# A planner's clock: other prices for the matrix products that set the order of two transformer blocks

## The chip, the cores and the metric

The kernel runs on one core of a Trainium2 chip. The metric is the device time of one execution in microseconds (us); a lower number is better. Engines are named as the profile names them: PE (matrix products; PEld is its weight load), DVE (element-wise work), ACT (activations, scaled copies), POOL (a few small operations) and SP, whose queue issues the loads.

## The reference

The input is 256 tokens of 1024 values in float32. Two blocks follow each other, each of two layers.

```python
def first_block(x, mem, ...):
    h = x
    for l in range(DEPTH):
        h = h + 0.5 * swiglu_ffn(rms_norm(h, ffn1_norm[l]), ffn1_w_in[l], ffn1_w_out[l])
        h = h + hybrid_mixer(rms_norm(h, mix_norm[l]), w_in[l], conv_w[l], ..., w_out[l])
        h = h + memory_cross_attention(rms_norm(h, xattn_norm[l]), rms_norm(mem, mem_norm[l]), ...)
        h = h + 0.5 * swiglu_ffn(rms_norm(h, ffn2_norm[l]), ffn2_w_in[l], ffn2_w_out[l])
    return rms_norm(h, final_norm)

def second_block(x, ...):                      # each layer:
    ...
    merged = g[:, :, 0] * y_moba + g[:, :, 1] * y_nsa + g[:, :, 2] * y_fox
    return x + merged @ w_out
```

The mixer of the first block has eight heads of stick-breaking attention and four heads of a gated delta rule (GDN) in chunks of 64 tokens, whose inputs pass a causal convolution. A layer of the second block has three attention branches: MoBA, NSA and FoX. NSA compresses keys and values: windows of 32 tokens pass a small network, `silu(flat @ w1) @ w2`. FoX needs a running sum of the logarithms of its forget gates.

## The kernel before, in words

All weights come from DRAM in float32 and are split into a high and a low part of the type f32r: ACT copies the high part (`wh<-raw`), DVE subtracts it from the raw value (`wl<-raw,wh`). Activations are split in the same way (for instance `uh`, `ul`). A dense product is three f32r matmuls, high by high, high by low and low by high (`mm3`, lines 603 to 605, and `chunk_T`, 623 to 628). Most have 256 columns (`pq`), those of the second block's inputs up to 512; the ones that the prediction speaks of have 384 (`pp`). Between these dense products stands side work: transposes (`pt`), sums and broadcasts by constant matrices (`rb`, `cum`), the attentions, the GDN chunks and the norms. Most of its matmuls on PE are float32.

The order on every engine is made by one planner when the program is built (class `Plan`, lines 205 to 335). It keeps a clock for each engine (`free`) and the planned time at which each tile is written (`note`, `ready`). The work of PE in order of the layers is a list; `dense` (598) runs one main product and then lets the side work go on. Each piece of side work is a generator that yields operations. An operation of DVE or ACT is emitted once its planned ready time and its engine's planned free time are near enough (`when`, 173; SLACK 0.25, QUEUE 0.6), a product of PE once 0.6 us have passed since its planned ready time (`PE_SLACK`). "Now" is the planned clock of PE. So what a product is priced at decides how many products are placed between a chain's operations. `until` and `wait` let the planned clock run on where the main product itself isn't ready; `hidden` (1710) waits in this way for the compressed windows `fs`.

The prices: a product has `c` of line 417, a transpose 0.11 us (423), DVE and ACT about 0.1 us plus the elements over a rate (`cost`, 246). Every operation goes through `Op.run` (185 to 193), so all rows of the profile carry line 193; after the change it is line 198.

Names in the rows: `fs` are the windows for NSA's compression, made from `kv` by a transpose (`pt`), DVE (`ft`) and ACT and DVE (`fs`); `hp` is their first product. `hss` are sums of squares of heads. `conv`, `cin` and `gz` belong to the first block's mixer. `fz`, `mz` and `nz` are the gated outputs of the three branches, transposed into `uh` and `ul`, from which `pq` of the branches' output products is made. `p` and `pT` are attention weights, `po` products with values. `lf` are FoX's logarithms, `cum` their running sum.

Of the kernel before, what the change touches and what calls it, by code (L numbers as in the profile page):

```python
# [11 lines left out]
F32R = mybir.dt.float32r  # L12
BF = mybir.dt.bfloat16
# [118 lines left out]
class Xt:  # L132


    def __init__(self, plan, hi, lo):
        self.plan, self.hi, self.lo, self.ready = plan, hi, lo, {}
# [23 lines left out]
class Op:  # L160


    def __init__(self, plan, eng, fn, args, kw, cost, late):
        self.plan, self.eng, self.fn, self.args, self.kw, self.cost, self.late = plan, eng, fn, args, kw, cost, late
        aps = [(i == 0 and "out" not in kw, v) for i, v in enumerate(args) if isinstance(v, bass.AP)]
        aps += [(k in ("out", "accum_out"), v) for k, v in kw.items() if isinstance(v, bass.AP)]
        self.outs = [v for o, v in aps if o]
        self.ins = [v for o, v in aps if not o]

    def ready(self):  # L170
# [14 lines left out]
    def run(self):  # L185
        pl = self.plan
        start = max(pl.free[self.eng], self.ready())
        end = start + self.price()
        pl.free[self.eng] = end
        pl.last = end + self.late  # L190
        for v in self.outs:
            pl.note(v, pl.last)
        return self.fn(*self.args, **self.kw)  # L193
# [13 lines left out]
class Plan:  # L207
# [8 lines left out]

    def __init__(self):
        self.free = {"T": 0.0, "V": 0.0, "A": 0.0, "G": 0.0, "D": 0.0}
        self.heap, self.seq, self.last = [], 0, 0.0
        self.writes = {}  # L220

    @property
# [127 lines left out]
def kernel(ctx: ExitStack, tc: tile.TileContext, a, out):  # L350
    nc = tc.nc
    T = nc.tensor
# [61 lines left out]

    def mm(o, lhsT, rhs, start=True, stop=True, skip=False):
        n = rhs.free_size()
        c = max(n, lhsT.free_size()) * (1 if lhsT.dtype in (F32R, BF) else 4) / 2400.0 + 0.002
        return Op(ck, "T", T.matmul, (), dict(out=o, lhsT=lhsT, rhs=rhs, start=start, stop=stop, skip_group_check=skip),
                  c, 0.2)

# [39 lines left out]
    def late_constants():  # L460
        load(cst[:, C_EARLY:], a["cst"][:, C_EARLY:])

        def run():
            yield V.tensor_tensor(fg, gain("final_norm", 0), gain("norm_g_2", 0), op=OP.mult)
            yield V.tensor_scalar(hbg, C(C_BG, 48), 0.5, None, op0=OP.mult)
            yield V.tensor_copy(idb, ident)
            yield A.activation(tri, C(C_LTN, 2 * P).rearrange("p (i n) -> p i n", i=2), AF.Copy)
            yield V.tensor_copy(sbn, C(C_SBN))
            yield V.tensor_copy(can, C(C_CAN))
        ck.spawn(run(), 0)  # L470
# [132 lines left out]
    def mm3(o, xh, xl, wh, wl, first, last):  # L603
        for lhs, rhs, a0, a1 in ((xh, wh, first, False), (xh, wl, False, False), (xl, wh, False, last)):
            dense(mm(o, lhs, rhs, a0, a1))
# [17 lines left out]
    def chunk_T(ps, n, wh, wl, xh, xl, first, last):  # L623
        for j in range(n // P):
            js = slice(j * P, (j + 1) * P)
            o = ps[j // 2][:, j % 2, :]
            for lhs, rhs, a0, a1 in ((wh, xh, first and j % 2 == 0, False), (wh, xl, False, False), (wl, xh, False, last)):
                dense(mm(o, lhs[:, js], rhs, a0, a1, skip=True))
# [58 lines left out]
    def token_sums(accs):  # L687

        n = len(accs)
        ps = yield from take("x", [P, n, 2], "ssq")  # L690
        for i in range(n):
            for t in range(2):
                yield mm(ps[:, i, t:t + 1], accs[i][:, t * P:(t + 1) * P], one1)
        r = [small("rs", (P, 2), 6) for i in range(n)]
        for i in range(n):
            yield V.tensor_scalar(r[i], ps[:, i, :], 1.0 / D, 0.0 if i else EPS, op0=OP.mult, op1=OP.add)
        give("x")
        return r
# [100 lines left out]
    def to_h(scale, nxt, nx=None):  # L799

        def done(n, ps):
            def run():
                if nx is not None:
                    rb = yield from nx.scale_b()
                for i in range(2):
                    b = 2 * n + i
                    hs = hT[:, 2 * b:2 * b + 2, :]
                    if nx is None:
                        yield V.scalar_tensor_tensor(hs, ps[i], scale, hs, op0=OP.mult, op1=OP.add)
                        give("a")  # L810
                    else:
                        d = k2([P, 2, S], "dh")
                        yield V.scalar_tensor_tensor(d, ps[i], scale, wide(rb), op0=OP.mult, op1=OP.mult)
                        give("a")
                        yield V.tensor_tensor(hs, hs, d, op=OP.add)
                    nxt.start(b)
            ck.spawn(run(), PR_H)
        return done


    def ffn(nx, w_in, w_out, nxt, between=None):
        act = Blocks()

        def block(n0, n):
# [3 lines left out]
            def gate(ps):  # L828
                def run():
                    rb = yield from nx.scale_b()  # L830
                    sg = st["sg"] = [k2([P, 2, S], "sg") for i in range(nk // 2)]
                    for i in range(nk // 2):
                        yield V.tensor_tensor(sg[i], ps[i], wide(rb), op=OP.mult)
                        give("a")
                        yield A.activation(sg[i], sg[i], AF.Silu)
                st["gate"] = ck.spawn(run())
# [1339 lines left out]
```

## Time and profile before

| | us |
|---|---|
| runs, median of three | 1848.15 (1847.22 to 1850.67) |
| profiled execution | 1848.62 |
| its span, first to last instruction | 1846.8 |
| PE busy | 1827.1 (99% of the span), 14854 instructions |
| DVE busy | 1256.0 (68%) |
| ACT busy | 988.2 (54%) |
| chain that ended last | PE 96%, DVE 2%, ACT 1%, issue 1% |

PE's busy time counts overlapping matmuls by their modelled ends: one product of 256 columns is shown with 0.28 us, though the next starts 0.12 us later. Times of single instructions on PE are therefore read from the distance of their starts. "x4" in a row of a timeline means four instructions in succession, and the bracket at its end is the idle time of that engine before them, with what released it. A float32 product that isn't a transpose is two instructions in the trace.

### The profile page before, as it was taken

The page shows a single profiled execution, that of the slowest core. Times are in us where ns is not written, and L with a number is a line of the kernel's source. Part 1 is how long each engine was busy: PE and PEld are TensorE (multiplying, and loading weights), DVE is VectorE, ACT ScalarE, POOL GpSimd, SP SyncE. Part 2 cuts the span into 40 slices and gives each one's busy share as a digit, 9 for nine tenths or more (in the row PEclk, how much of TensorE's full clock was granted, in tenths as well). Part 3 has the DMA queues.
Part 4 walks back from the last instruction along what each step waited for, and adds up shares of the span by engine and source line. Part 5 has one row for each costly group of instructions (what it writes and reads, how often), then busy time and mean ns, then how long its engine had stood idle before and what let it go on. Part 6 is the DMA issues. An engine that isn't in the chain of part 4 may idle for free.

```text
span 1846.8 us, 35541 instructions
## 1 busy us (share of the span) xinstructions
PE 1827.1 (99%) x14854; PEld 1768.2 (96%) x14854; DVE 1256.0 (68%) x2083; ACT 988.2 (54%) x1648; POOL 70.6 (4%) x72
## 2 busy tenths in 40 slices
PE   8999999999999999999999999999999999999999
PEld 8999999899999999999998899999989999999998
DVE  6557687675655565576866666556777868787686
ACT  5446375454544444464654545444576654666553
POOL 0000001000000000000010000000110000101000
PEclk9999999999999999999999999999999999999999
DMA  7546463244554555464632445546535625545533
GB/s 256 183 147 236 144 206 115 92 144 130 183 183 160 188 190 184 146 236 150 203 123 92 137 138 172 184 155 199 168 113 164 234 87 182 166 122 173 198 108 127
DMA packets 169581, 300.90 MB, mean 163 GB/s; under 512 B 7884, under 2 KB 51020, under 8 KB 169292
## 3 DMA queue, kind: packets, MB, share of 16 engines
q1 hardware_dynamic: 169420, 298.63, 50.3%
q8 instruction: 116, 1.90, 0.4%
q14 instruction: 45, 0.37, 0.1%
HBM read 297.56 MB, written 1.05 MB: 162 GB/s over the span
## 4 chain that ended last, share of the span: by engine, by line
PE 96%; DVE 2%; ACT 1%; issue 1%; DMA 0%; POOL 0%; SPq 0%; ACTq 0%; POOLq 0%
PE pq L193 69%; PE pp L193 14%; PE pt L193 2%; PE s L193 1%; PE z L193 1%; PE po L193 1%; PE xs L193 1%; PE xo L193 1%; PE hp L193 1%; DVE wl L193 1%; PE mp L193 1%; PE ep L193 1%; PE sbo L193 1%; ACT wh L193 0%; DMA raw<-in_ffn_w_in_dram 0%
## 5 line engine op out<-in xcount | busy, mean ns | idle before, releaser
L193 DVE TENSOR_TENSOR wl<-raw,wh 128x1024 fp32r<-128x1024 f32 (+3 forms) x628 | 689.3, 1103 | 383.9 <-ACT wh L193 380.9
L193 ACT ACTIVATE wh<-raw 128x1024 fp32r<-128x1024 f32 (+3 forms) x628 | 598.6, 962 | 512.8 <-PE pq L193 384.8
L193 PE MATMUL pq<-ffn_normh,wh 128*128 128x256 f32 x1408 | 399.7, 284 | 0.1
L193 PE MATMUL pq<-ffn_norml,wh 128*128 128x256 f32 x1408 | 399.5, 284 | 0.0
L193 PE MATMUL pq<-ffn_normh,wl 128*128 128x256 f32 x1408 | 399.5, 284 | 0.0
L193 PEld LDWEIGHTS pq<-ffn_normh,wh 128*128 128x128 f32 x1408 | 271.2, 193 | 0.5 <-ACT ffn_normh L193 0.5
L193 PEld LDWEIGHTS pq<-ffn_norml,wh 128*128 128x128 f32 x1408 | 271.2, 193 | 0.0
L193 PEld LDWEIGHTS pq<-ffn_normh,wl 128*128 128x128 f32 x1408 | 271.1, 193 | 0.0
L193 PE MATMUL pq<-ah,wh 128*128 128x256 f32 x704 | 199.5, 283 | 0.0
L193 PE MATMUL pq<-al,wh 128*128 128x256 f32 x704 | 199.5, 283 | 0.0
L193 PE MATMUL pq<-ah,wl 128*128 128x256 f32 x704 | 199.3, 283 | 0.0
L193 PEld LDWEIGHTS pq<-ah,wl 128*128 128x128 f32 x704 | 135.1, 192 | 0.2 <-DVE wl L193 0.2
L193 PEld LDWEIGHTS pq<-al,wh 128*128 128x128 f32 x704 | 135.1, 192 | 0.0
L193 PEld LDWEIGHTS pq<-ah,wh 128*128 128x128 f32 x704 | 135.1, 192 | 0.0
L193 PE MATMUL pp<-wh,norm_g_2l 128*128 128x384 f32 (+3 forms) x352 | 118.9, 338 | 0.0
L193 PE MATMUL pp<-wl,norm_g_2h 128*128 128x384 f32 (+3 forms) x352 | 118.4, 336 | 0.3 <-DVE wl L193 0.3
L193 PE MATMUL pp<-wh,norm_g_2h 128*128 128x384 f32 (+3 forms) x352 | 118.0, 335 | 0.0
L193 PE MATMUL pq<-norm_g_2h,wl 128*128 128x256 f32 x384 | 110.7, 288 | 0.4 <-DVE wl L193 0.4
L193 PE MATMUL pq<-norm_g_2h,wh 128*128 128x256 f32 x384 | 110.5, 288 | 0.0
L193 PE MATMUL pq<-norm_g_2l,wh 128*128 128x256 f32 x384 | 109.7, 286 | 0.0
L193 PE MATMUL pq<-mix_normh,wl 128*128 128x256 f32 x320 | 91.4, 286 | 0.5 <-DVE wl L193 0.5
L193 PE MATMUL pq<-mix_normh,wh 128*128 128x256 f32 x320 | 91.7, 286 | 0.0
(428 smaller groups left out, 3776.5 us busy)
## 6 DMA issues: line engine op xcount, KB each, us to landing
raw<-in_ffn_w_in_dram SPq DMA_DIRECT2D x79, 1024.0 KB, 5.2
raw<-in_w_in_dram SPq DMA_DIRECT2D x48, 1024.0 KB, 5.1
raw<-in_ffn_w_out_dram SPq DMA_DIRECT2D x40, 1024.0 KB, 5.2
raw<-in_w_in_dram SPq DMA_DIRECT2D x28, 768.0 KB, 4.4
raw<-in_xattn_w_kv_dram SPq DMA_DIRECT2D x16, 1024.0 KB, 5.1
raw<-in_w_out_dram SPq DMA_DIRECT2D x16, 1024.0 KB, 5.1
raw<-in_ffn_w_in_dram SPq DMA_DIRECT2D x18, 512.0 KB, 3.7
raw<-in_xattn_w_q_dram SPq DMA_DIRECT2D x8, 1024.0 KB, 5.1
```

Of the source, the lines that this page charges most:

```text
L193: return self.fn(*self.args, **self.kw)
```

## The change

Two prices of PE are altered; nothing that is computed is.

A product's price was the larger of its columns and its weights' columns, over 2400 per us, plus 0.002, with a factor of 4 for float32. Now it is its columns alone, with the same factor, plus 0.014, and at least 0.112. That makes 0.121 from 0.109 for f32r of 256 columns, 0.174 from 0.162 for 384, 0.227 from 0.215 for 512 and for float32 of 128, 0.112 from 0.055 for f32r of 64 to 128 columns with as many weights, and for float32 with 64 columns and 128 of weights 0.121 from 0.215. Besides, each product of PE whose last operand is of another kind (f32r or bfloat16 on the one side, the rest on the other) than that of the product before it is priced 0.06 higher.

```diff
@@ Op.__init__
         self.outs = [v for o, v in aps if o]
+        self.kind = aps[-1][1].dtype
         self.ins = [v for o, v in aps if not o]
@@ Op.run
         end = start + self.price()
+        if self.eng == "T":
+            small = self.kind not in (F32R, BF)
+            end += 0.06 * (small != pl.small)
+            pl.small = small
         pl.free[self.eng] = end
@@ Plan.__init__
-        self.heap, self.seq, self.last = [], 0, 0.0
+        self.heap, self.seq, self.last, self.small = [], 0, 0.0, False
@@ mm
-        c = max(n, lhsT.free_size()) * (1 if lhsT.dtype in (F32R, BF) else 4) / 2400.0 + 0.002
+        c = max(n * (1 if lhsT.dtype in (F32R, BF) else 4) / 2400.0 + 0.014, 0.112)
```

The instructions are the same in number and kind; 631 of the program's products are now priced with the added 0.06. Their order moves throughout. Three places follow.

The first is the first layer of the second block, where the windows of NSA are made. On PE, before:

```order
L193 MATMUL po<-fv,pT 128x128
L193 MATMUL pt<-cst,kv 128x128 x2
L193 MATMUL po<-fv,pT 128x64
L193 MATMUL po<-fv,pT 128x128
L193 MATMUL po<-fv,pT 128x64
L193 MATMUL po<-fv,pT 128x128
L193 MATMUL po<-fv,pT 128x64
L193 MATMUL po<-fv,pT 128x128
L193 MATMUL po<-fv,pT 128x64
L193 MATMUL pt<-cst,kv 128x128 x2
L193 MATMUL hp<-wh,fs 30x256
```

And the same place of PE now, with the dense products `pp` of 384 columns between:

```order
L198 MATMUL pt<-cst,kv 128x128 x2
L198 MATMUL pp<-wh,norm_g_2h 128x384
L198 MATMUL pp<-wl,norm_g_2h 128x384
L198 MATMUL pp<-wh,norm_g_2l 128x384
...
L198 MATMUL pt<-cst,kv 128x128 x2
L198 MATMUL pp<-wh,norm_g_2l 128x384
...
L198 MATMUL hp<-wh,fs 30x256
```

Eight `pp` now stand between the two pairs of `kv` and thirteen between the second and `hp`; the seven `po` stand elsewhere. In the second layer it is eight and seven. On DVE the same place read, before:

```order
L193 TENSOR_TENSOR wl<-raw,wh 128x2x384
L193 TENSOR_TENSOR ft<-pt,cst 64x240 x2
L193 RECIPROCAL sums<-sums 128x2
L193 TENSOR_REDUCE hss<-hsq 128x6
L193 TENSOR_TENSOR fz<-fz,sums 128x128
L193 TENSOR_REDUCE ut<-po 128x128
L193 TENSOR_REDUCE hss<-hsq 128x6
L193 TENSOR_TENSOR fs<-ft,fs 128x16x15
```

And now:

```order
L198 TENSOR_TENSOR wl<-raw,wh 128x2x256
L198 RECIPROCAL sums<-sums 128x2
L198 TENSOR_TENSOR fz<-fz,sums 128x128
L198 TENSOR_REDUCE ut<-po 128x128
L198 TENSOR_SCALAR ngt<-ngt 128x24
L198 TENSOR_TENSOR ft<-pt,cst 64x240 x2
L198 TENSOR_TENSOR fz<-ut,fz 128x128
L198 TENSOR_TENSOR wl<-raw,wh 128x2x256
L198 TENSOR_TENSOR fs<-ft,fs 128x16x15
```

The two `hss` no longer stand between `ft` and `fs`; one `fz` and one `wl` do.

The second place is the first block's mixer, on DVE, from the third weight split of 2x264 on. Before:

```order
L193 TENSOR_TENSOR wl<-raw,wh 128x2x264
L193 SCALAR_TENSOR_TENSOR conv<-cin,cst,conv 128x253
L193 SCALAR_TENSOR_TENSOR conv<-cin,cst,conv 128x254
L193 SCALAR_TENSOR_TENSOR conv<-cin,cst,conv 128x255
L193 TENSOR_SCALAR conv<-cin,cst 128x256
L193 TENSOR_TENSOR wl<-raw,wh 128x2x264
L193 SCALAR_TENSOR_TENSOR conv<-cin,cst,conv 128x253
L193 SCALAR_TENSOR_TENSOR conv<-cin,cst,conv 128x254
L193 TENSOR_TENSOR wl<-raw,wh 128x1024
```

And now:

```order
L198 TENSOR_TENSOR wl<-raw,wh 128x2x264
L198 TENSOR_SCALAR conv<-cin,cst 128x256
L198 SCALAR_TENSOR_TENSOR conv<-cin,cst,conv 128x253
L198 SCALAR_TENSOR_TENSOR conv<-cin,cst,conv 128x254
L198 SCALAR_TENSOR_TENSOR conv<-cin,cst,conv 128x255
L198 TENSOR_SCALAR conv<-cin,cst 128x256
L198 SCALAR_TENSOR_TENSOR conv<-cin,cst,conv 128x253
L198 TENSOR_TENSOR wl<-raw,wh 128x2x264
L198 SCALAR_TENSOR_TENSOR conv<-cin,cst,conv 128x254
L198 TENSOR_TENSOR wl<-raw,wh 128x1024
```

One `conv` stands between the last 2x264 split and that of 1024 where two stood; more of them stand ahead of it. On ACT one `cin` more stands ahead of the high part of that last 2x264 split than before.

The third place is the end of a second-block layer on PE, where the gated outputs are transposed for the branches' output products. Before:

```order
L193 MATMUL pt<-cst,fz 128x128 x3
L193 MATMUL pt<-cst,p 128x128 x4
L193 MATMUL po<-vcat,pT 128x64
...
L193 MATMUL po<-vcat,pT 128x64
L193 MATMUL pq<-uh,wh 128x256
L193 MATMUL pt<-cst,mz 128x128 x3
L193 MATMUL pq<-ul,wh 128x256
```

And now:

```order
L198 MATMUL pq<-norm_g_2h,wh 128x256
L198 MATMUL pq<-norm_g_2l,wh 128x256
L198 MATMUL pq<-norm_g_2h,wl 128x256
L198 MATMUL pt<-cst,fz 128x128 x6
L198 MATMUL pq<-uh,wh 128x256
L198 MATMUL pt<-cst,mz 128x128 x3
L198 MATMUL pq<-ul,wh 128x256
```

The four `p` and the seven `po` (five of them are left out above) no longer stand between the transposes of `fz` and the first `pq` of `uh`.

## Rows read from the trace of the kernel before

**Rows 1.** The page, part 1: busy time, share of the span, instructions.
```profile
PE 1827.1 (99%) x14854; PEld 1768.2 (96%) x14854; DVE 1256.0 (68%) x2083; ACT 988.2 (54%) x1648; POOL 70.6 (4%) x72
```
**Rows 2.** PE's waits by releaser: us in total, times, longest.
```profile
PE pt L193 <- DMA h<-in_x_dram: 7.1, 3, 4.3
PE hp L193 <- DVE fs L193: 2.6, 2, 1.6
PE sp L193 <- DVE vn L193: 1.4, 2, 0.7
PE pt L193 <- DVE ft L193: 0.9, 2, 0.6
PE pq L193 <- DVE wl L193: 0.9, 4, 0.2
PE cum L193 <- DVE lf L193: 0.8, 1, 0.8
PE pt L193 <- DVE pT L193: 0.5, 1, 0.5
PE po L193 <- DVE ut L193: 0.4, 2, 0.2
```
**Rows 3.** Windows: us, busy PE, PEld, DVE, ACT, POOL, PEclk, DMA share, GB/s.
```profile
660.00:720.00 60.00, 60.00 (x503) 60.00 (x502) 39.26 (x47) 28.81 (x35) 0.69 (x1) 1.00 0.57 184
1380.80:1384.20 3.40, 3.40 (x14) 3.37 (x12) 3.33 (x11) 1.83 (x3) 2.84 (x1) 0.51 0.30 54
1418.00:1441.00 23.00, 22.81 (x184) 21.73 (x183) 19.28 (x43) 17.50 (x41) 1.64 (x1) 1.00 0.56 179
```
**Rows 4.** Timeline of PE, first layer of block two: start, us, form, idle before.
```profile
1376.37 0.44 PE L193 MATMUL pt<-cst,kv 128*128 128x128 f32 x2 [0.45 <-DVE pT L193]
...
1378.06 0.41 PE L193 MATMUL pt<-cst,kv 128*128 128x128 f32 x2 [0.55 <-DVE ft L193]
1380.04 0.30 PE L193 MATMUL hp<-wh,fs 128*30 128x256 f32 x1 [1.57 <-DVE fs L193]
```
**Rows 5.** Timeline of DVE at the same place.
```profile
1379.13 0.54 DVE L193 TENSOR_REDUCE hss<-hsq 128x6 f32<-128x384 f32 x1
1379.59 0.40 DVE L193 TENSOR_TENSOR fs<-ft,fs 128x240 fp32r<-128x240 f32 x1
```
**Rows 6.** Timeline of PE, second layer of block two.
```profile
1644.27 0.41 PE L193 MATMUL pt<-cst,kv 128*128 128x128 f32 x2 [0.39 <-DVE ft L193]
1645.73 0.30 PE L193 MATMUL hp<-wh,fs 128*30 128x256 f32 x1 [1.05 <-DVE fs L193]
```
**Rows 7.** Timeline of PE, first norm: the broadcast rb between dense products.
```profile
30.11 0.60 PE L193 MATMUL rb<-cst,rs 128*128 128x128 f32 x4
...
30.67 0.28 PE L193 MATMUL pq<-ffn_normh,wh 128*128 128x256 f32 x1
```
**Rows 8.** Timeline of PE behind the first hp: products of 384 columns.
```profile
1381.12 0.53 PE L193 MATMUL pp<-wh,norm_g_2h 128*128 128x384 f32 x1
...
1384.00 0.46 PE L193 MATMUL pp<-wh,norm_g_2h 128*128 128x384 f32 x1
```
**Rows 9.** Timelines of DVE and ACT in the first mixer.
```profile
239.18 0.71 DVE L193 TENSOR_TENSOR wl<-raw,wh 128x528 fp32r<-128x528 f32 x1 [1.11 <-ACT wh L193]
239.81 0.99 DVE L193 SCALAR_TENSOR_TENSOR conv<-cin,cst,conv 128x253 f32<-128x253 f32 x2
240.75 1.23 DVE L193 TENSOR_TENSOR wl<-raw,wh 128x1024 fp32r<-128x1024 f32 x1
...
239.05 0.71 ACT L193 ACTIVATE cin<-conv 128x256 f32<-128x256 f32 x2
```
**Rows 10.** Timelines of PE and ACT before the first uh of block two.
```profile
1513.28 0.52 PE L193 MATMUL pt<-cst,fz 128*128 128x128 f32 x3
...
1514.77 0.36 PE L193 MATMUL pq<-uh,wh 128*128 128x256 f32 x1
...
1513.84 0.49 ACT L193 ACTIVATE uh<-pt 128x384 fp32r<-128x384 f32 x1 [0.55 <-PE pt L193]
```

## The prediction

> **What bounds the kernel now.** I read the page's busy times first: PE is busy for 1827.1 of the span's 1846.8 us [rows 1]. So the only time to be had is where PE stands, runs at the lower clock, or does other work. The second view was the list of PE's waits by releaser [rows 2]. 7.1 us are the load of x at the start, which the change doesn't touch. Behind it the waits are short and nearly all on DVE: 2.6 us for fs, 1.4 for vn, 0.9 for ft, 0.9 for wl, 0.8 for lf, 0.5 for pT, 0.4 for ut. Third came the table of windows: a stretch of plain dense products runs 503 of them in 60 us at granted clock 1.00, and one stretch of 3.4 us stands at 0.51, half speed [rows 3]. Last I read the timelines at the two longest waits.
>
> Both are at one place, the compressed keys of NSA in the two layers of the second block. In the first layer PE transposes a first pair of kv after a wait of 0.45 us, a second pair after 0.55, and stands 1.57 for fs [rows 4]. Ahead of fs on DVE stand two reductions of hss, the second from 1379.13 [rows 5]. In the second layer the waits are 0.39 and 1.05 [rows 6]. A wait is counted from the modelled end of the matmul before it, which is later than the next could have started: the pair at 1378.06 is two products at a pitch of about 0.11, so hp could have started at 1378.28 and came at 1380.04, 1.76 later instead of the 1.57 shown. The same correction, about 0.17, belongs to each of the five.
>
> **What the change does to the clock.** It computes nothing anew. It alters what the planner believes PE's products to last, and by that the order. Measured pitches are the yardstick.
>
> Products of 256 columns: 60 us over 503 is 0.119 [rows 3]. The old price is 256/2400 + 0.002 = 0.109, the new one 0.121. The old clock ran 9% slow in a plain stretch, so a chain of side work that it gave 2.5 us of products really got 2.76; now it gets 2.49. The first effect, then, is that every hop of a chain has about 0.27 us less cover.
>
> The Trainium skill has a rule on this, "TensorE: Matmul & The Clock Gate", section "Back-to-back issue gap": an isolated product at full clock takes N/2.4 + 2.5 ns. An estimate from it is 109 ns at 256 columns, the old price; by it the old clock was right and the new one runs 10% fast. The trace disagrees, with 0.119 measured, so I give this no chance of its own; it would only make the thinner cover below larger.
>
> Changes of kind: rb, four small f32 products between dense f32r ones, starts at 30.11, one dense product follows it, and the next starts at 30.67 [rows 7]. Four at 0.11 and one at 0.12 make 0.56, all of the distance. The trace has nothing for the 0.06 that the change books at each of two transitions. The order has 631 such changes, so the plan books 38 us that PE doesn't spend, all of it where side work is dense. Those hops lose cover beyond the 0.27.
>
> **The sum, against the profiled execution's 1848.6 us** (the median of the runs is 1848.15, 0.5 lower).
>
> First, kv and hp. The rows of the order show that in the first layer the second pair of kv now stands 13 products of 384 columns ahead of hp, where it stood directly before it, and the first pair 21 ahead. At 0.12 x 384/256 = 0.18 each (an estimate from the 0.119), 21 are 3.7 us of cover beside the transposes. What fs needs from the first pair was 3.5 us before (1376.37 to 1379.9) with two hss of 0.5 ahead of it; the order has taken them away from there, which leaves 2.5. So that wait goes. In the second layer only 15 products stand between the first pair and hp, 2.7 us against the same 2.5: nearly all of it goes. The products that came between, po, run elsewhere at the same cost. Gain: 0.45 + 0.55 + 1.57 + 0.39 + 1.05 = 4.0, with five corrections of 0.17 4.85; I take 0.3 off for the second layer's narrow cover: **-4.55**. Bounds: 0, if DVE's wl ahead of fs comes late each time, to -4.85.
>
> Second, the clock. In the stretch behind the stall the granted clock is 0.51, the lower level of 1.2 GHz [rows 3]. PE had been standing for most of two microseconds. Products of 384 columns are 0.32 apart there, nine of them from 1381.12 to 1384.00 [rows 8], against 0.18: 9 x 0.14 = 1.3. Without the stall it goes: **-1.3** (0 to -1.3; the second layer has the stall and no fall).
>
> Third, the mixers. Before, DVE idles 1.11 at 239.18 for ACT's wh, splits wl of 528, does two conv, and only then the wl of 1024 columns at 240.75 [rows 9] that PE waits for. The order now puts only one conv, 0.40, between the two, and one more cin, 0.33, ahead of that wh on ACT. The wl comes 0.1 to 0.2 earlier, in two mixers: **-0.3**. The bounds are -0.5, two of the 0.2 waits for wl [rows 2], and +0.7, two cin with nothing hidden. The conv moved forward fall into that idle time; without it they cost 0.4 each.
>
> Fourth, lf. PE waits 0.8 for it in one layer [rows 2]. Between that layer's rb and cum the order leaves 27 products of 384 columns instead of 29, so the wait grows by 2 x 0.18: **+0.35** (0, if the chain starts earlier with its rb, to 0.7).
>
> Fifth, uh. Before, three transposes of fz at 1513.28 are followed by four of p and seven po; pq starts at 1514.77, and ACT's uh runs from 1513.84 for 0.49 [rows 10]. Now all six transposes of fz stand directly ahead of pq. These are 0.66 us, and uh needs 0.56 + 0.49 from the first of them: a new wait of 0.4 in each layer. Before, the distance from pq to pq around the transposes behind it already held some of that, so I take half: **+0.45** for both layers (0 to 0.9).
>
> Sixth, thinner cover everywhere else. Nothing in the trace prices it directly. Nine waits of the list [rows 2] (wl, ft, pT, ut) lie between 0.1 and 0.6 and make 2.7 us. If places lie as densely just on the other side, four more turn into waits per 0.27, each by half of it: 0.6. With a little for the 0.06 I take **+0.8**. Bounds: 0, to 0.6 plus all nine growing by 0.27, 3.0.
>
> The two waits for vn stay: the order has the chain of GDN in the same hops. POOL, SP and the loads keep their sequence, and the weight streams are 0.57 busy on DMA in a plain stretch [rows 3]. The number of products of each kind is unchanged.
>
> Sum: -4.55 - 1.3 - 0.3 + 0.35 + 0.45 + 0.8 = -4.55, so 1844.1 in a profile and **1843.5 us** as a median.
>
> **Rivals.**
> A, the gain is handed back: fs comes early, but the thinner cover costs its upper bound, 3.0 instead of 0.8, and uh and lf theirs, 0.9 and 0.7. For it: hops with transposes lose both 0.27 and the unpaid 0.06, and [rows 2] shows how many places lie just late. Against it: no hop lies wholly in islands. Net -4.55 - 1.3 - 0.3 + 0.7 + 0.9 + 3.0 = -1.55, a median of 1846.5.
> B, slower: side work that the fast clock emits earlier lands on DVE ahead of weight splits. The place is the attention of the second block, 1418 to 1441 and its twin in the other layer, where DVE is busy 19.28 of 23 us [rows 3]. Ten per cent of that, 1.9 us, moves ahead of a wl. It decides where the moved work exceeds the idle time directly ahead of that wl: 3.7 us stand in the whole stretch, but spread over several gaps. Then PE waits 1.9 twice, with a half-clock stretch of 1.3 behind each, 6.4, and the mixers' 0.7 + 0.3 come on top: 1843.5 + 7.4 = 1851. For it: PE waits for wl at four places already [rows 2]. Against: DVE's own prices are not altered.
> C, the nearer clock also frees the short waits for wl, ut, pT and ft elsewhere: 0.9 + 0.4 and the 0.8 of lf, with 0.17 on each of seven, and the thinner cover costs nothing: -4.55 - 1.3 - 2.1 - 1.2 = -9.2, 1839.
> D, the change does nothing, because order alone moves and PE's sum is the same: 1848. For it: PE is 99% busy. Against: the waits of fs stand in the trace and the order moves just them.
>
> **How the numbers follow.** Forecast 0.50, A 0.20, B 0.14, C 0.11, D 0.05. A measurement of this kernel tells about 0.2% from no change, 3.7 us. The forecast's own range is 1841.5 to 1845.5, a fifth of it above 1844.45, so faster is 0.40 + 0.11 + 0.02 of A = 0.53; the same is 0.10 + 0.18 + 0.05 = 0.33; slower is 0.14. The range that leaves a tenth on each side reaches from C's 1839, a little below for its unpaid places, to near B: 1838 to 1850.
>
> **What would show it.** In the changed kernel's list of PE's waits hp<-fs should be below 0.5 and the kv transposes gone; there should be no stretch of clock 0.5 behind the first. cum should wait about 1.2, and pq of uh appear with some 0.4. The wait for wl at the mixers should not grow. Wrong would be the sum if PE's waits on wl together exceed 3 us (B), if waits under 0.3 us multiply (A), or if hp still waits over 1 us.

## The result: slower by 1%, and the profile after

The changed kernel takes 1867.9 us in the median of four runs (1866.2 to 1870.6) beside 1848.6 for the one before: a ratio of 1.0104, with an interval of 1.0093 to 1.0116. Forecast were 1843.5 and a range of 1838 to 1850. The prediction was wrong in direction.

The page after, part 1, answers to [rows 1]:

```profile
PE 1836.0 (98%) x14854; PEld 1770.9 (95%) x14854; DVE 1261.4 (68%) x2083; ACT 988.6 (53%) x1648; POOL 70.3 (4%) x72
```

The instructions are as many as before, and the span grew from 1846.8 to 1864.4, so the 17.6 us more are PE standing and PE at the lower clock. The waits of PE answer to [rows 2]; of those up to 0.5 us only the one of cum is shown (us in total, times, longest):

```profile
PE pt L198 <- DMA h<-in_x_dram: 6.9, 3, 4.0
PE qs L198 <- DVE csq L198: 2.7, 2, 1.4
PE pt L198 <- DVE Sn L198: 2.2, 2, 1.1
PE pt L198 <- DVE ul L198: 2.1, 2, 1.0
PE pp L198 <- DVE wl L198: 2.1, 5, 0.8
PE sp L198 <- DVE vn L198: 1.4, 2, 0.7
PE pq L198 <- DVE wl L198: 1.3, 2, 0.6
PE pq L198 <- ACT uh L198: 1.3, 2, 0.6
PE pp L198 <- ACT wh L198: 0.9, 2, 0.4
PE pt L198 <- DVE qh L198: 0.7, 3, 0.2
...
PE cum L198 <- DVE lf L198: 0.3, 1, 0.3
```

The waits of hp for fs and of pt for ft are gone from the list, 3.5 us, and new ones stand in their place. All waits listed make 23.8 us in 36 places, before 15.1 in 19: 8.7 more, and 2.9 more for the 17 additional places at 0.17 each, the correction that the prediction worked out.

The rest is the clock. These windows of the changed kernel (columns as in [rows 3]) stand behind the waits for csq and for ul:

```profile
255.30:258.00 2.70, 2.70 (x13) 2.70 (x14) 1.23 (x1) 0.98 (x2) 0.00 (x0) 0.50 0.00 0
1531.00:1534.00 3.00, 3.00 (x16) 3.00 (x16) 1.62 (x3) 1.01 (x2) 0.00 (x0) 0.52 0.00 0
1800.00:1803.00 3.00, 3.00 (x16) 3.00 (x16) 1.62 (x3) 1.37 (x3) 0.00 (x0) 0.52 0.00 0
1376.00:1384.00 8.00, 8.00 (x59) 7.58 (x57) 7.06 (x20) 5.65 (x17) 0.63 (x1) 1.00 0.33 98
```

Three stretches run at the lower level of 1.2 GHz (0.50 and 0.52); the one that the kernel before had behind hp is gone (last row). The clock doesn't fall in every run of one kernel, so runs are compared below in two parts as well: span times granted clock, an estimate of the time that the span would take at full clock, and the rest. The clock is listed to three places, so a single run's part is good to 0.9 us, a mean of several to less. Before (84 runs, taken beside the experiments): 1843.3 + 3.6. After (4 runs): 1857.1 + 9.3. So about 13.7 us are waits and 5.7 the clock.

Where they arise follows from the starts of the same dense product in both traces, each less the pitches of all products ahead of it. A pitch is the usual distance of two starts where PE neither stands nor runs at the lower clock; the rows are good to some 0.3.

| stretch | us gained (-) or lost |
|---|---|
| up to the first mixer | +0.3 |
| first mixer, projections | +5.5 |
| rest of that layer | +0.6 |
| FFNs between, with the memory's transposes | +0.2 |
| second mixer, projections | +2.4 |
| rest of that layer | +0.6 |
| second block, layer 1, up to the last product ahead of hp | +1.4 |
| from there to hp | -3.0 |
| the clock behind hp | -1.6 |
| from there to the first product of uh | +3.7 |
| the first products of uh | +3.1 |
| layer 2, up to the last product ahead of hp | -0.3 |
| from there to hp | -1.8 |
| from there to the first product of uh | +3.7 |
| the first products of uh | +3.0 |
| the end | -0.2 |

The place that was forecast to gain did so: in layer 1, 4.52 us lay between the starts of the last product ahead of hp and of hp before, and 0.17 lie there now.

```profile
1375.52 0.34 PE L193 MATMUL pp<-wh,norm_g_2l 128*128 128x384 f32 x1
1387.89 0.34 PE L198 MATMUL pp<-wh,norm_g_2l 128*128 128x384 f32 x1
```

### The profile page after: what moved, and what is told of

Read it like the earlier page. It is cut to its first block, busy times and chain, and to the rows that moved or that the text cites. A ratio compares the mean times of both kernels' runs of the same rounds, so it can differ in the third digit from the quotient of the medians.

```text
span 1864.4 us, 35555 instructions
## 1 busy us (share of the span) xinstructions
PE 1836.0 (98%) x14854; PEld 1770.9 (95%) x14854; DVE 1261.4 (68%) x2083; ACT 988.6 (53%) x1648; POOL 70.3 (4%) x72
## 4 chain that ended last, share of the span: by engine, by line
PE 88%; DVE 7%; ACT 2%; issue 1%; POOL 1%; DMA 0%; SPq 0%; POOLq 0%; ACTq 0%
PE pq L198 65%; PE pp L198 11%; PE pt L198 2%; DVE wl L198 2%; PE z L198 1%; PE s L198 1%; DVE conv L198 1%; ACT wh L198 1%; PE po L198 1%; PE xs L198 1%; PE xo L198 1%; PE mp L198 1%; PE ep L198 1%; POOL hss L198 1%; PE sbo L198 1%
```

## The experiments

Where an edit starts from "before" or "after", that is the kernel before or the changed one. F32r products of 256 columns and more are called dense. Ratios are to the kernel before, on the same chip, with 95% intervals.

**Price or fee?** Four kernels. The first two take the change apart.

```diff
# e1_price, from after
-            end += 0.06 * (small != pl.small)
+            end += 0.0 * (small != pl.small)
# e2_fee, from after
-            end += 0.06 * (small != pl.small)
+            end += 0.05 * (small != pl.small)
-        c = max(n * (1 if lhsT.dtype in (F32R, BF) else 4) / 2400.0 + 0.014, 0.112)
+        c = max(n, lhsT.free_size()) * (1 if lhsT.dtype in (F32R, BF) else 4) / 2400.0 + 0.002
# e3_cover, from after
-    PE_SLACK = -0.6
+    PE_SLACK = -0.9
# e5_traced, from e1_price
+        if lhsT.dtype not in (F32R, BF):
+            c = 2 * max(0.11, n / 1200.0)
+            if lhsT.shape[0] <= 64 or lhsT.free_size() <= 64:
+                c = 0.06 if n <= 64 else 0.112
```

> The changed kernel with the new price of products and without the 0.06 for a change of kind. Theory P (the price does the harm: before, products priced 9% too low gave every chain about that much real cover, which made up for what the plan leaves out on ACT and DVE): the waits of the mixers and of uh are all here, the time is 1860 to 1868. Rival F (the fee does the harm: the trace shows no such cost, so the plan's clock runs 38 us ahead where side work is dense): most of the loss is gone, 1846 to 1852. Rival R (any other order costs about this much, since the order before was picked among many): somewhere between 1853 and 1866, with waits at other places than in the changed kernel.

Measured: 1869.3 us, ratio 1.0101 (1.0074 to 1.0128), as slow as the changed kernel, 1 above theory P's range and outside those of F and R.

> The kernel before with its old price of products and a fee for a change of kind, 0.05 instead of 0.06. Theory P: mixers and uh as before, PE waits for kv and hp moved, 1844 to 1851. Rival F: 1858 to 1867, thinner cover wherever side work is dense. Rival R: 1853 to 1866.

Measured: 1847.4, ratio 0.9991 (0.9982 to 1.0001). By itself the fee costs nothing, though by the trace it is false. Theory F falls: without the new prices of products there is no harm. Rival R's range is missed here as well, so not every other order costs that much.

> The changed kernel with PE_SLACK at -0.9 instead of -0.6: side products stand 0.3 us of planned time later on PE. Theory P: this gives back what the nearer price took from hops of 2.5 to 3 us; uh, qs and the short waits of side products go, while the mixers' wait of dense products for wl (an order of ACT and DVE, which PE_SLACK doesn't touch) stays: 1847 to 1853. Rival F: part of it, 1853 to 1860. Rival R: 1853 to 1866 with waits at new places.

Measured: 1861.4, ratio 1.0060 (1.0043 to 1.0077), 1852.1 at full clock and 7.0 for the clock. The cover of side products gave back 5 of the 13.7 us of waits and 2 of the clock. Theory P's number is missed, F's by 1, and R's is met; pp still waits 1.8 for wl, as it said, but so does qs for csq, 2.2, and ul grew to 3.4.

> Prices as the trace has them: f32r as in the changed kernel, float32 of 128 columns 0.22, of 64 rows or columns 0.06 to 0.112, and no fee. Theory P: the mixers' waits (qs for csq, pp for wl and wh) are as in the changed kernel, 8 us; with uh as before, since the order has the seven po between there again: 1855 to 1863. Rival F: the truest clock gives the best order, 1842 to 1848. Rival R: 1853 to 1866, elsewhere.

Measured: 1860.0, ratio 1.0058 (1.0043 to 1.0073). The prices nearest to the trace, without a fee, are slower than the false ones before. Theory P's range holds, and R's with it.

**The mixer's cin.** The trace after shows on ACT what holds up the first mixer:

```profile
234.69 0.65 ACT L198 ACTIVATE wh<-raw 128x528 fp32r<-128x528 f32 x1 [0.73 <-PE pp L198]
236.55 0.42 ACT L198 ACTIVATE cin<-conv 128x256 f32<-128x256 f32 x1 [1.21 <-DVE conv L198]
236.87 2.98 ACT L198 ACTIVATE gz<-pp,rs 64x128 f32<-64x128 f32 x8
239.86 0.42 ACT L198 ACTIVATE cin<-conv 128x256 f32<-128x256 f32 x1
240.19 2.52 ACT L198 ACTIVATE wh<-raw 128x528 fp32r<-128x528 f32 x3
```

and on PE what follows from it:

```profile
240.87 0.39 PE L198 MATMUL pp<-wh,mix_normh 128*128 128x264 f32 x1 [0.45 <-ACT wh L198]
241.61 0.39 PE L198 MATMUL pp<-wl,mix_normh 128*128 128x264 f32 x1 [0.35 <-DVE wl L198]
...
251.53 0.38 PE L198 MATMUL qs<-one,csq 128*128 128x1 f32 x2 [1.36 <-DVE csq L198]
```

One cin has come ahead of the eight gz. It waits 1.21 us for DVE's conv, and gz, wh and wl wait behind it. Before, ACT read here:

```profile
234.35 0.65 ACT L193 ACTIVATE wh<-raw 128x528 fp32r<-128x528 f32 x1 [0.62 <-PE pp L193]
235.49 2.98 ACT L193 ACTIVATE gz<-pp,rs 64x128 f32<-64x128 f32 x8 [0.49 <-PE pp L193]
238.50 0.65 ACT L193 ACTIVATE wh<-raw 128x528 fp32r<-128x528 f32 x1
```

gz itself waited 0.49 for PE there, so not all of the 1.21 is new. Counted from the wh ahead, gz now starts 1.04 later (2.18 for 1.14), and the wh of the last split of 2x264, with a second cin ahead of it, 1.35 later (5.50 for 4.15). wl follows, then DVE's csq, and with the clock behind it the mixer loses 5.5 us. The next kernels add a planner's wait for both halves of conv:

```diff
# x1_cin from after, y4_d012_cin from x2_dense, y3_d006_cin from x5_d006: in conv_done
                         if j % 2:
+                            yield Wait(ck.ready(co[:, j - 1:j + 1, :]) - ck.SLACK)
# x2_dense, from before (x5_d003 and x5_d006: 0.003 and 0.006)
+        if lhsT.dtype == F32R and n >= 256:
+            c += 0.012
```

In three pairs of kernels with the same prices (after and x1_cin, x2_dense and y4_d012_cin, and further below w2_after_oldf32 and w1_x1_oldf32) the edit moves in each of the two mixers two instructions of ACT, so that one cin stands behind gz and another behind a weight split, and five products of PE, among them the first qs; the order of DVE is the same.

> The changed kernel with one more planner's wait in the mixer: the first silu that writes cin is emitted only when both halves of conv are planned ready, so that on ACT it stands behind the eight gz instead of ahead of them. Theory H (in the mixers the harm is one ACT instruction that stands ahead of gz, waits 1.2 us on DVE's conv and holds back gz, wh, wl and csq): the waits of pp for wh and wl and most of qs for csq go, the lower clock behind them too; 1868 falls by 5 to 9, to 1859 to 1863. Rival W (the mixers lose since every weight split has less cover): the waits stay or move, 1866 or more.

Measured: 1862.6, ratio 1.0074 (1.0059 to 1.0089), 5.3 less than the change, in theory H's range; W falls. At full clock 1854.3, 2.7 less; the clock's part is 6.0, 3.3 less. On ACT cin now stands behind gz, which starts without that wait:

```profile
235.16 3.00 ACT L198 ACTIVATE gz<-pp,rs 64x128 f32<-64x128 f32 x8 [0.49 <-PE pp L198]
238.17 0.72 ACT L198 ACTIVATE cin<-conv 128x256 f32<-128x256 f32 x2
```

The waits of pp for ACT's wh are gone, those of qs for csq fell from 2.7 to 1.8 only, and in the run whose trace this is the clock falls in the second mixer instead of the first:

```profile
240.00:300.00 60.00, 59.05 (x578) 55.15 (x579) 50.66 (x89) 31.47 (x60) 6.56 (x6) 1.00 0.50 160
904.00:908.00 4.00, 4.00 (x21) 4.00 (x20) 1.69 (x2) 2.10 (x4) 0.00 (x0) 0.50 0.15 20
```

> The kernel before with 0.012 more on f32r products of 256 columns and more, and nothing else. Theory P (the price of dense products alone sets it): cin stands ahead of gz in the order again and the mixers lose their 7 to 10 us; kv and hp wait less; the end of a layer has po beside uh and loses little: 1855 to 1862. Rival S (the prices of small products matter as much): 1847 to 1852.

Measured: 1853.6, ratio 1.0028 (1.0017 to 1.0039), between the ranges of P and S: 1846.5 and 5.3. The true price of dense products alone brings about a quarter of the loss.

> The kernel before with 0.012 more on dense products, as in x2_dense, and the planner's wait that puts cin behind gz. Theory H: the mixers' waits of pp for wh and wl go; qs may still wait 1 us for csq in each mixer, and where it does the lower clock may follow. 1846 to 1851, from 1853.6. Rival W: no better than x2_dense, 1852 to 1855.

Measured: 1847.9, ratio 0.9996 (0.9987 to 1.0005). In theory H's range; W falls. With the cin back the dense price costs nothing net. It isn't harmless elsewhere: by the reckoning of the table this kernel gains 3.0 and 1.8 at the two hp, as the changed one does, and 0.7 behind the first, and loses most of it again in other places.

**How much, and which small products.** The dense price by half and by a quarter, and the new price for one kind of small products at a time, on the kernel before, on y4_d012_cin and on x5_d006:

```diff
# x3_f32 from before, z3_y4_f32 from y4_d012_cin, y1_d006_f32 from x5_d006
+        if lhsT.dtype not in (F32R, BF):
+            c = max(n * 4 / 2400.0 + 0.014, 0.112)
# x3_r from before, z2_y4_r from y4_d012_cin
+        if lhsT.dtype in (F32R, BF) and n < 256:
+            c = max(n / 2400.0 + 0.014, 0.112)
# y2_after_d006, from after
+        if lhsT.dtype == F32R and n >= 256:
+            c -= 0.006
```

> The same with half of it, 0.006. In the order cin stands behind gz here. Theory H with thresholds (single instructions that change places do the harm): the mixers lose nothing against before, kv and hp wait less, 1845 to 1850. Rival L (thinner cover costs in proportion to the price): about half of x2_dense's loss, 1851 to 1856.

Measured: 1842.7, ratio 0.9968 (0.9955 to 0.9981): faster than both kernels and below the ranges of H and L, 1839.9 at full clock and 0.7 for the clock. Its list of PE's waits:

```profile
PE pt L193 <- DMA h<-in_x_dram: 6.6, 3, 3.8
PE hp L193 <- DVE fs L193: 2.1, 2, 1.1
PE pq L193 <- DVE wl L193: 0.8, 2, 0.4
PE pt L193 <- ACT cin L193: 0.6, 2, 0.3
PE pp L193 <- DVE wl L193: 0.5, 2, 0.3
PE kS L193 <- DVE Sn L193: 0.4, 2, 0.2
PE cum L193 <- DVE lf L193: 0.4, 1, 0.4
```

Besides the load of x these are eleven waits instead of sixteen. hp still waits for fs, yet those of the kv transposes and the lower clock behind hp are gone: by the reckoning of the table 2.0 us of the 5.9 that this trace is shorter lie at the two hp and 1.6 in the clock behind the first. Some 0.7 in each of four other places, the GDN and the uh of both layers, make most of the rest.

> The kernel before with 0.003 more on dense products. Theory H: no harmful place flips in the order (cin behind gz; three fz and then pq of uh, with p and mz behind); kv and hp wait less: 1843 to 1849. Rival L: midway between 1848.4 and the 1842.7 of 0.006, or, if the time is as good as random in the price, outside 1843 to 1849.

Measured: 1849.9, ratio 1.0006 (0.9997 to 1.0016). With 1848.4, 1849.9, 1842.7 and 1853.6 at 0, 0.003, 0.006 and 0.012 the time doesn't follow the price in either direction. So rival L falls in its first form, and theory H's range is missed by 1; what L named last, a time as good as random in the price, is met.

> The kernel before with the new price for float32 products alone (0.012 more for 128 columns, about half for 64 columns with 128 of weights). Theory P: no dense price is altered, the mixers' first place is as before, 1845 to 1852. Rival S: 1854 to 1862.

Measured: 1845.2, ratio 0.9983 (0.9974 to 0.9993), in theory P's range; S falls.

> The kernel before with the new price of small f32r products alone. Theory Q: 1853 to 1860, with waits in the attentions of both blocks. Rival A: 1845 to 1851.

Measured: 1852.6, ratio 1.0026 (1.0015 to 1.0037): between the two, on Q's side.

> y4_d012_cin (dense products 0.012 dearer, cin behind gz; 1847.9) with the new price of f32r products under 256 columns as well. Theory Q (the small f32r price, which holds for the products of the attentions, takes filler away from the tails of the chains): 1855 to 1862. Rival A (only all three prices together make the order with six fz ahead of pq of uh, which isn't in this order): 1846 to 1851.

Measured: 1849.2, ratio 1.0006 (0.9996 to 1.0015), in rival A's range: theory Q falls. The price that cost 4 us on the kernel before costs 1 here.

> y4_d012_cin with the new price of float32 products instead. Theory Q: little changes, 1846 to 1851. Rival A: the same, 1846 to 1851. Rival G (the float32 price, too low by half for products of 64 columns with 128 of weights, makes the loss once the dense price is true): 1854 to 1862.

Measured: 1856.8, ratio 1.0046 (1.0031 to 1.0061). The price that gained 3 us on the kernel before loses 9 here, as rival G said, with the clock's part unchanged (1.9 in both). Part of it is in the GDN, where y4_d012_cin has no such rows:

```profile
PE kS L193 <- DVE Sn L193: 1.8, 2, 0.9
...
PE vp L193 <- DVE X L193: 1.5, 2, 0.7
```

> Two settings that were each faster than before, together: dense products 0.006 dearer and float32 products at the new price. Theory H: the places add up only where they differ; both gain at kv and hp, so 1839 to 1843. Rival (any gain is an accident of one order): 1844 to 1850.

Measured: 1848.8, ratio 0.9997 (0.9987 to 1.0006): two settings that each gained make none together. The rival holds.

> The changed kernel, fee and all, with 0.006 taken off the price of f32r products of 256 columns and more. In the order cin stands behind gz, but the six fz stand directly ahead of pq of uh. Theory H (two places do most of the harm, each by the order of a few instructions): the mixers lose at most 2 us against before; the end of each layer of the second block still loses about 4, with the lower clock behind it; kv and hp gain 2 to 4: 1849 to 1855. Rival L (cover in proportion to the price): half the loss at both places, and the end of a layer not more than 2 each: 1856 to 1860.

Measured: 1857.4, ratio 1.0044 (1.0029 to 1.0059): 1853.7 and 1.9. Most of the clock's part is gone, a quarter of the waits. Theory H's range is missed, and rival L's is met: here taking off half of the dense price takes off about half of the loss. The waits that stay are many and short, though cin stands behind gz.

> x5_d006 (1842.7) with the planner's wait for cin, whose first place differs little in the order. Theory H: within 2 us of x5_d006, 1841 to 1845. Rival (each change of order is as good as random): 1845 to 1852.

Measured: 1845.3, ratio 0.9980 (0.9971 to 0.9989), just outside theory H's range and in the rival's. The edit costs 2.6 where cin stands well already, but it isn't the same small move: here some 45 instructions of DVE change places in the mixers, where none did in the three pairs.

**Do the places add up?** The end of a layer of the second block looks like this after. On PE:

```profile
1526.81 0.82 PE L198 MATMUL pt<-cst,fz 128*128 128x128 f32 x6
1528.26 0.38 PE L198 MATMUL pq<-uh,wh 128*128 128x256 f32 x1 [0.63 <-ACT uh L198]
1529.69 0.55 PE L198 MATMUL pt<-cst,mz 128*128 128x128 f32 x3 [1.04 <-DVE ul L198]
```

and on DVE, where two gt stand ahead of ul:

```profile
1527.48 0.68 DVE L198 TENSOR_TENSOR gt<-pq,rsb 128x512 f32<-128x512 f32 x1
...
1528.28 0.68 DVE L198 TENSOR_TENSOR gt<-pq,rsb 128x512 f32<-128x512 f32 x1
...
1529.08 1.02 DVE L198 TENSOR_TENSOR ul<-pt,uh 128x384 fp32r<-128x384 f32 x2
```

The last two kernels take the old float32 price:

```diff
# w1_x1_oldf32 from x1_cin, w2_after_oldf32 from after
+        if lhsT.dtype not in (F32R, BF):
+            c = max(n, lhsT.free_size()) * 4 / 2400.0 + 0.002
```

> x1_cin (1862.6) with the old price for float32 products. Beside z2_y4_r (1849.2) it has the fee and, through it, the six fz directly ahead of pq of uh. Theory U (that place costs about 4 in each layer, whatever the other prices): waits of pq for ACT's uh and of mz for ul, the lower clock behind them, 1855 to 1859. Rival G (the float32 price makes the rest of the loss, the place is harmless without it): 1847 to 1852.

Measured: 1860.0, ratio 1.0055 (1.0038 to 1.0071): 1856.0 and 2.8. Above theory U's range by 1, and not for its reason. The waits at that place are there (1.3 for uh, 1.5 for ul), yet the clock doesn't fall behind them; in this trace it falls in both mixers, of which the first is shown:

```profile
240.00:300.00 60.00, 58.54 (x538) 54.96 (x536) 47.51 (x84) 29.52 (x58) 6.56 (x6) 0.94 0.49 159
1430.00:1545.00 115.00, 112.56 (x913) 107.61 (x912) 88.14 (x185) 66.65 (x140) 3.44 (x2) 1.00 0.47 155
```

Beside z2_y4_r this kernel has the fee and, on 48 bfloat16 products of 256 columns and more, 0.012 more; nothing else. On the old prices the fee cost nothing; on these the two cost 10.7 us, for which the 48 products, 0.6 us of planned time, weren't tried alone.

> The changed kernel with the old price for float32 products; cin stands ahead of gz. Theory H with U (places add up): w1_x1_oldf32 plus the 5.5 that cin cost twice, 1860 to 1865. Rival G: 1852 to 1857.

Measured: 1868.1, ratio 1.0099 (1.0084 to 1.0114): 1857.8 and 7.9. Slower than both theories said. The cin are here worth 8.2 us, of which 1.8 are waits and 5.1 the clock (the rest is the difference of median and mean); in the other two pairs it was 5.7 and 5.3. Taking back the float32 price gained the changed kernel nothing, so rival G falls here.

Of the eighteen kernels of this section three are faster than the kernel before with an interval clear of 1, five are the same within it and ten slower. So rival R, by which any other order costs about as much, doesn't hold as it stands; that the order before was a lucky one among many isn't excluded, and nothing here tells ahead of a run which order will be a good one.

## Why the prediction was wrong

By its own steps:

- **First, kv and hp: right.** It gave -4.55, and by the table the two places gained 3.0 and 1.8. The trace after has no wait of hp for fs. The pairs of kv stand ahead, and fs is written 1.4 us before hp starts; [rows 4] and [rows 5] are answered by

```profile
1383.89 0.44 PE L198 MATMUL pt<-cst,kv 128*128 128x128 f32 x2
1385.56 0.38 PE L198 MATMUL pt<-cst,kv 128*128 128x128 f32 x2
1388.06 0.28 PE L198 MATMUL hp<-wh,fs 128*30 128x256 f32 x1
...
1386.21 0.40 DVE L198 TENSOR_TENSOR fs<-ft,fs 128x240 fp32r<-128x240 f32 x1
```

  The same 3.0 and 1.8 were gained by x2_dense, y4_d012_cin and e2_fee, none of which is faster than before: each time the rest of the new order took most of it back.
- **Second, the clock: right there, wrong elsewhere.** It gave -1.3; the clock is 1.00 around kv and hp, worth 1.6. But three other stretches fell, each behind a new wait. The prediction let the clock's gain in and priced no new fall except in rival B.
- **Third, the mixers: the step that failed first.** It said -0.3, with +0.7 as the bound, "two cin with nothing hidden". It priced the cin that came ahead on ACT by how long it runs, 0.33. Here it held up what stood behind it on ACT by what it waited for: 1.21 for conv, of which 0.49 had been a wait for PE before, so that gz came 1.04 and wh 1.35 later, and wl and csq after them. The mixers lost 5.5, with the clock, and 2.4 us. Three pairs of kernels (x2_dense and y4_d012_cin, after and x1_cin, w2 and w1) show 5.3 to 8.2 for the two cin of each mixer, both mixers together; from after to x1_cin it was 2.7 of waits and 3.3 of clock. About 1 us of waits in each mixer stays without them.
- **Fourth, lf: wrong in direction.** +0.35 forecast; the wait shrank from 0.8 to 0.3, and it is in the other layer now.
- **Fifth, uh: mis-sized.** +0.45 forecast, 0.9 as the bound; the place cost 3.1 and 3.0. The wait of pq for uh came as it was worked out, 0.63 a layer, and it stands in all kernels with fz directly ahead of pq (after, e1_price, x1_cin, y2, w1, w2, and x5_d003 with three fz) and in no other. The step left out ul behind two gt on DVE, 1.0 a layer, and the clock behind both. The wait for ul doesn't come from the six fz: e2_fee, with eight po between fz and pq, has it as well, and its clock is 1.000 over the whole run:

```profile
PE pt L198 <- DVE ul L198: 2.1, 2, 1.0
...
core 0: 1845.5 us, clock 1.000
```

  No run takes this place alone out of the changed kernel, and in w1_x1_oldf32 the same order there brought no lower clock.
- **Sixth, thinner cover: the largest miss.** +0.8, with 3.0 as the bound. What is neither in the mixers' projections nor at hp and the clock behind it nor at uh comes to 10.0 by the table, most of it short waits in the second block. The pairs show how much this hangs on the rest: the new float32 price makes -3.2, +6.1, +8.8, +2.7 and -0.2 us on five sets of other prices (before, x5_d006, y4_d012_cin, w1, w2), the fee -1.2, +10.7 (with the 48 products) and, on e1_price, -1.4. No bound from single rows of before could hold that.

So three terms of the sum failed: the mixers (7.9 measured for -0.3), uh (6.1 for 0.45) and the cover (10.0 for 0.8). In its small sums the prediction has 2.76 and 2.49 where 0.119 gives 2.73 and 2.46, fs done at 1379.9 where the row has 1379.99, and a fifth of its own range above 1844.45 where it is a quarter; none of these matters beside the three.

Of the rivals, B had the direction and the mechanism, side work that is emitted early and lands ahead of weight splits with a lower clock behind it, but its place was second, its price 7.4, and the chance 0.14. The forecast followed the two longest waits of before and gave every other place a small average.

Shown is: the harm is in the prices of products, not in the fee by itself; the cin are worth 5 us and more; the clock makes about 5.7 of the 19.3. Open is the rest, some 11 us of waits net of what kv and hp gained (13.7 less the 2.7 that went with cin): no single price makes them, and they come only in combination. That a falser price gave cover is argued, not shown: e3_cover gave back 5 of 13.7, which fits it but is another order too, and 0.006, which is truer than before, is faster.

## What to carry to other kernels

When a planner's prices are altered, read in the new order which instruction now stands ahead of which on each in-order engine, and price it by when its input is ready, not by how long it runs alone. A truer price in one place isn't a gain by itself where the plan is false in others; treat it as a setting, try a few values, and measure. On a PE that is 99% busy, count for each new wait of a microsecond the lower clock that may follow it.

## What was not expected of the hardware

The clock can fall behind waits of little more than 1 us: behind 1.36 for csq it stood at 0.50 in a window of 2.7 us. It need not: e2_fee waits 1.03 for ul in each layer, and its clock is 1.000 over the run. And it isn't the same from run to run: four runs of w1_x1_oldf32 had granted clocks of 0.996, 1.000, 1.000 and 0.998 with spans of 1862.8, 1856.9, 1856.2 and 1859.4. Multiplied, all four come to between 1855.3 and 1856.9, so nearly all of that spread is the clock.
